# Attention in a hybrid block: ACT's casts and bank copies ahead of the exponentials, other places for a modulation sum, for output products and for weight splits

## The chip, the cores and the metric

The kernel runs on 1 core of one Trainium2 chip. The metric is the time of one execution on the device in microseconds (us), median of 3 runs. The engines are named as the profile names them: PE (TensorE, matmuls; PEld its weight loads), DVE (VectorE), ACT (ScalarE), POOL (GpSimd) and SP (SyncE, which issues the DMAs here). Each engine works its own queue in order, and engines wait for one another by semaphores.

## The reference, cut to what matters

One layer of a flow-matching block on 512 latent tokens with 256 context tokens as a prefix, model width 1024, all in float32. The input projection is split into three groups of heads: grouped-query attention, a long convolution, and differential attention.

```python
sh1, sc1, g1, sh2, sc2, g2 = split(silu(c) @ w_mod + b_mod, 6)     # csh1 ... from c_ctx
h  = modulate(rms_norm(x, norm1_g), sh1, sc1);  hc = modulate(rms_norm(ctx, norm1_g), csh1, csc1)
qa, ka, va, hy, qd, kd, vd = split(h @ w_in)                       # and the same of hc
# attention: 4 query heads on 2 key heads; keys and values = context (256) + latent (512) = 768
ya = softmax(qa ka^T / 8) va
# differential attention: 4 heads, two 64-wide halves j, values 128 wide
yd = softmax(q1 k1^T / 8) vd - lam * softmax(q2 k2^T / 8) vd
yh = hyena(hy)                                                     # long convolutions
y  = concat(rms_norm(ya), rms_norm(yh), rms_norm(yd) per head * 0.2) @ w_out
x  = x + g1 * y
x  = x + g2 * conv_glu(modulate(rms_norm(x, norm2_g), sh2, sc2))
```

## The kernel before, in words

Matmuls that need more than one pass's accuracy split both operands into a rounded high part and a low part and add three products (`mm3`): `hi_of` makes the high part by a cast, mostly on ACT, `lo_of` the low part by a subtraction on DVE or POOL.

*Order.* The layer that the kernel is written in plans each engine's order from program order and a planning model. Where the code enters `tc.manual_schedule(engines=...)`, the named engines run the instructions traced inside in exactly the order of the code; instructions traced outside may be planned between them. `tc.issue_after(ins)` queues what is traced in it behind `ins` on the engine of `ins`. Buffers (`bufs=`) of one tag are reused; which one a new tile gets is fixed by the planner, and its first write waits for the last use of the tile before.

*Modulation sums.* The four vectors g1, sh2, sc2, g2 are sums over 8 row blocks of `w_mod`. A call of `mod2_step` (L746) loads one block (512 KB, two buffers) and adds it, scaled, to a running sum on DVE (`macc`, L761, L763). After the eighth block of a group the next call does nothing (`pause`), and the call after that closes the sum first (`due`: 16 small matmuls on PE into `mc`, L768, one add on DVE into `mcol`, L769) and then loads the next group's first block. Calls stand in the loop over the input projection's eight column chunks: `MOD_AT` calls ahead of each half chunk, 22 in all, in chunks 1 to 6 (`ci`), and in the last chunk (`ci == 7`) at places `e` of its twelve groups of matmuls. In the last chunk PE and DVE are ordered by hand, and six early score tiles of head 0 (`early_step`: scores `se`, maximum `mxe`, exponential `pe`) run between the projection's matmuls.

*Attention.* From L1160 a loop runs over steps n. Steps 3 to 15 here are the differential heads (4 heads x 4 query tiles; 0 to 2 were the early ones), 16 to 31 the grouped-query heads. PE, DVE and ACT are ordered by hand. A step below `LATE` = 16 does, in this order: scores of half 0 on PE into one of two score banks `s`, row maximum on DVE, exponential on ACT; `combine` of step n-1 (DVE and POOL mix the two probabilities); `advance`; three transposes of the first half of step n-3's probabilities on PE into one of three banks (`ps_t`), a copy of that bank on ACT (`at`); scores, maximum, exponential of half 1; the other three transposes and their copy; the products with the values of step n-5 (`yd`); `advance` again. `advance` lets each running side job do its next piece: preparing the next head's q and k (transposes `qT`, `kT` on PE, casts `qhl`, `kh` on ACT, low parts on DVE, DMAs that stack them), finishing a head (`ysb`, `natural` = transposes `ynd`, copy, squares, norm), splitting the grouped-query values (`vas`), and writing an output operand (`y_out`: transposes `yT`, cast `Y` on ACT, low part on DVE). These side jobs use the same three transpose banks. In the trace a name such as `Td21` is head 2, query tile 1.

*End of the attention and output projection.* After the loop, `TAIL` says how many output products (`accumulate`, one product = three matmuls of 512 columns into `o`) go to PE ahead of each further `advance`. The advances finish the grouped-query heads: `natural`, scaling (L1022), squares, reduction (L1028), reciprocal root on POOL, scaling of `yna` (L1037), transposes `yTa`, `Y` cast and low part, twice. The 24 products that need neither `Y[0]` nor `Y[1]` are spread over these places; the rest follow at once. Weight units 0 to 7 of `w_out` (`wo_unit`: load `or`, cast `oh` or `ox`, low part `ol` or `ox`) alternate: units 0 to 2 are split during the loop, 3 to 7 are traced behind the hand-ordered part; the letter of `WO_LO` says whether POOL or DVE makes the low part. Loads of raw units share three buffers, which later hold the gate weights `ur` too. Then come g1 spread over the rows (`mr`), the last products, the residual sum on x, the second norm and the gated MLP.

Of the kernel before, what the change touches and what calls it, by code (L numbers as in the profile page):

```python
# [8 lines left out]
F32 = mybir.dt.float32  # L9
F32R = mybir.dt.float32r  # L10
AF = mybir.ActivationFunctionType
ALU = mybir.AluOpType
AX = mybir.AxisListType
# [3 lines left out]
P = 128  # L17
WO_LO = "ppppvvvv"

# [7 lines left out]
WO_AT = (24, 26, 28)  # L27
TAIL = (2, 0, 0, 0, 0, 0, 7, 0, 0, 2)
UP_AT, UP_AHEAD, UP_NEXT, UP_LAG = 4, 5, 5, 2
# [15 lines left out]
def block_kernel(tc, x, ctxt, small, ffs, wmod1, wmod2, whyd, wqkvd, woutd, wupd, wdownd,  # L45
# [700 lines left out]
    def mod2_step():  # L746

        if m2s.pop("pause", False):
            return
# [14 lines left out]
        if k == NK - 1:  # L764
            def due(a=m2s["a"]):
                t0 = m2s["ps"](f"mc{g}")
                for i in range(NK):
                    T_.matmul(t0[:, 2 * i:2 * i + 2], a[:, i * P:(i + 1) * P], ones[:, 0:2], start=True, stop=True)  # L768
                V.tensor_tensor(mcol[:, g], t0[:, 0:16:2], cols[:, C_BM + 8 * g:C_BM + 8 * g + 8], ALU.add)  # L769
            m2s["due"], m2s["pause"] = due, True  # L770

    def scores(s, qs, ks, kz, j, tt):

        q2 = qs[:, j, tt * P:(tt + 1) * P]
        for c0, c1 in ((0, 512), (512, 768)):
            T_.matmul(s[:, c0:c1], q2, ks[j][:, c0:c1], start=True, stop=False)
            T_.matmul(s[:, c0:c1], q2, kz[j][:, c0:c1], start=False, stop=True)

    def exp_of(p_, mx, s, stat):
        V.tensor_reduce(mx, s[:, :768], AX.X, ALU.max, negate=True)  # L780
        S.activation(p_, s[:, :768], AF.Exp, bias=mx, scale=1.0, accum_out=stat)
# [10 lines left out]
    def early_step(e):  # L792
        n, jj = divmod(e, 2)
        if n >= EARLY:
            return
        qs, (ks, kz) = prepared[0]["q"], prepared[0]["k"]
        s = pp(f"se{n}{jj}")
        scores(s, qs, ks, kz, jj, n)
        if jj:
            p_ = big(f"pe{n}{jj}")[:, :768]  # L800
        else:
            p_ = f(rows_of(y_tile(f"pe{n}{jj}"), 768))
            held[n] = []
        mx = cst.tile([P, 1], F32, tag="mxe", bufs=2, name=f"mxe{n}{jj}")
        exp_of(p_, mx, s, state["st0"][:, n, jj:jj + 1])
        held[n].append(p_)
# [10 lines left out]
    for ci, ch in enumerate(corder):  # L817
# [6 lines left out]
        for u in range(2):  # L824
# [8 lines left out]
            for b, bank in enumerate(banks):  # L833
                th, tl = (hTh, hTl) if b < 2 else (cTh, cTl)
                for j in range(2):
# [6 lines left out]
                    if ci == 7:  # L842
# [3 lines left out]
                        if e in (4, 8):  # L846
                            early_mix(e // 4 - 1)
                        if e % 3 == 0:
                            mod2_step()
# [164 lines left out]
    def finish_a(b, yps):  # L1014
# [15 lines left out]
        if b == 1:  # L1030
# [4 lines left out]
            for b_ in range(2):  # L1035
                yv = yna[b_].rearrange("p a j d -> p a (j d)")
                V.tensor_tensor(yv, yv, sa[:, 2].unsqueeze(2).broadcast_to([P, 4, P]), ALU.mult)  # L1037
                yield
                yield from y_out(b_, f"a{b_}", lambda tt: yv[:, tt])
# [7 lines left out]
    def front(n, jj):  # L1047
# [3 lines left out]
        if kind == "a":  # L1051
            if jj:
                return lambda: []
            stat, j_ = sta[:, tt, 2 * h + j:2 * h + j + 1], j
# [8 lines left out]
        def rest():  # L1063
            mx = att.tile([P, 1], F32, tag="mx", bufs=4, name="mx" + nm)
            p_ = att.tile([P, 768], F32, tag="p", bufs=7, name="p" + nm)
            exp_of(p_, mx, s, stat)
            return [p_]
        return rest
# [61 lines left out]
    def wo_unit(n_):  # L1130
# [9 lines left out]
        hi_of(h, r, "a")  # L1140
        lo_of(l, r, h, WO_LO[n_])
        wo[n_] = h.rearrange("p (k c) -> p k c", k=2), l.rearrange("p (k c) -> p k c", k=2)
# [22 lines left out]
    while n < len(steps) + D_V:  # L1165
# [10 lines left out]
        if late:  # L1176
# [4 lines left out]
            if n - 1 in waiting:  # L1181
                held[n - 1] = waiting.pop(n - 1)()
            if on(D_C):
# [8 lines left out]
        else:  # L1192
            held[n] = front(n, 0)()
            if on(D_C):
                combine(n - D_C, held[n - D_C])
            advance()
            if on(D_T):
                transposes(n - D_T, held[n - D_T][0], 0)
            held[n] += front(n, 1)()
            if on(D_T):  # L1200
                transposes(n - D_T, held.pop(n - D_T)[0], 1)
            if on(D_V):
                values(n - D_V)
# [303 lines left out]
```

## Time and profile before

| | before |
|---|---|
| median of 3 runs | 807.86 us (805.63 to 809.38) |
| the profiled execution: its time | 807.56 us |
| the profiled execution: span, first to last instruction | 805.8 us |
| PE busy | 774.5 us (96%) |
| DVE, ACT, POOL busy | 476.9, 317.8, 194.6 us |

The profile is of one execution. Its span is 1.8 us shorter than that execution's time. A busy PE is not PE at its peak, but where PE is not busy it waits, and the rows of the trace name for whom. Times in the rows are microseconds from the start of the span.

### The profile page before, as it was taken

What the parts mean: (1) busy time and instruction counts of PE and PEld (TensorE: products, weight loads), DVE (VectorE), ACT (ScalarE), POOL (GpSimd) and SP (SyncE); (2) the same over time, 40 slices, a digit from 0 to 9 for tenths busy, and PEclk for the clock granted to TensorE, in tenths of its full rate; (3) what the DMA queues carried; (4) which work ended last, traced back from release to release, by engine and by line L of the source; (5) the groups of instructions that cost most, each with busy time, mean ns of one, the idle gap of its engine ahead of it and who ended that gap; (6) DMA issues with size and microseconds to landing.
All of it is one profiled execution on the core that took longest, in us unless ns stands there. A gap on an engine that the chain in (4) does not pass through costs nothing.

```text
span 805.8 us, 11143 instructions
## 1 busy us (share of the span) xinstructions
PE 774.5 (96%) x4355; PEld 655.1 (81%) x4355; DVE 476.9 (59%) x683; ACT 317.8 (39%) x546; POOL 194.6 (24%) x187
## 2 busy tenths in 40 slices
PE   8899999999989888899899999999999999999997
PEld 2278899999988777789689988888888888888886
DVE  5588659687767777776476785344444433332325
ACT  2576343223213678787243343323333332332220
POOL 0518036849821657421151000000000000000000
PEclk9799999999999999999999999999999999999999
DMA  8913311225675241501551372322232222223202
GB/s 325 393 51 112 105 54 53 79 79 179 214 218 161 66 104 29 144 27 53 171 171 54 113 245 86 105 104 83 101 105 90 93 99 84 100 85 104 79 27 104
DMA packets 30701, 93.68 MB, mean 116 GB/s; under 512 B 5639, under 2 KB 8022, under 8 KB 29625
## 3 DMA queue, kind: packets, MB, share of 16 engines
q1 hardware_dynamic: 30649, 92.98, 35.0%
q8 instruction: 34, 0.56, 0.3%
q14 instruction: 18, 0.15, 0.1%
HBM read 83.79 MB, written 2.10 MB: 107 GB/s over the span
## 4 chain that ended last, share of the span: by engine, by line
PE 81%; DVE 6%; DMA 4%; ACT 4%; POOL 2%; issue 1%; SPq 0%; ACTq 0%; DVEq 0%; POOLq 0%
PE u L84 5%; PE u L83 5%; PE u L85 5%; PE dn L85 5%; PE dn L84 5%; PE dn L83 5%; DMA mraw<-in_dram 4%; PE uv L83 2%; PE ua L85 2%; PE uv L84 2%; PE uv L85 2%; PE ua L83 2%; PE ua L84 2%; PE yd L1103 2%; PE o L85 2%; PE o L84 2%
## 5 line engine op out<-in xcount | busy, mean ns | idle before, releaser
L80 DVE TENSOR_TENSOR ul<-ur,uh 128x1024 fp32r<-128x1024 f32 x62 | 75.9, 1224 | 101.6 <-ACT uh L72 100.9
L72 ACT CAST uh<-ur 128x1024 fp32r<-128x1024 f32 x66 | 69.2, 1051 | 116.8 <-PE u L84 90.6
L83 PE MATMUL u<-h2h,uh 128*128 128x512 f32 (+1 forms) x224 | 81.3, 363 | 0.0
L85 PE MATMUL u<-h2h,ul 128*128 128x512 f32 (+1 forms) x224 | 80.4, 359 | 0.0
L84 PE MATMUL u<-h2l,uh 128*128 128x512 f32 (+1 forms) x224 | 80.4, 359 | 0.0
L84 PE MATMUL dn<-ul,gh 128*128 128x512 f32 x176 | 69.6, 397 | 0.0
L85 PE MATMUL dn<-uh,gl 128*128 128x512 f32 x176 | 69.6, 397 | 0.0
L83 PE MATMUL dn<-uh,gh 128*128 128x512 f32 x176 | 69.3, 397 | 0.0
L80 DVE TENSOR_TENSOR gl<-gT,gh 128x512 fp32r<-128x512 f32 x22 | 15.2, 690 | 60.1 <-ACT gh L72 60.1
L84 PEld LDWEIGHTS u<-h2l,uh 128*128 128x128 f32 x224 | 42.3, 189 | 6.3
L83 PEld LDWEIGHTS u<-h2h,uh 128*128 128x128 f32 x224 | 42.3, 189 | 6.2
L85 PEld LDWEIGHTS u<-h2h,ul 128*128 128x128 f32 x224 | 42.3, 189 | 6.2
L80 DVE TENSOR_TENSOR wl<-wr,wh 128x1024 fp32r<-128x1024 f32 x22 | 31.5, 1433 | 19.4 <-ACT wh L72 19.3
L763 DVE SCALAR_TENSOR_TENSOR macc<-mraw,sv,macc 128x1024 f32<-128x1024 f32 x28 | 37.4, 1335 | 8.1 <-DMA mraw<-in_dram 8.0
L72 ACT CAST gh<-gT 128x512 fp32r<-128x512 f32 x22 | 13.5, 620 | 70.1 <-PE dn L84 70.1
L83 PEld LDWEIGHTS dn<-uh,gh 128*128 128x128 f32 x176 | 33.2, 189 | 8.1
L85 PEld LDWEIGHTS dn<-uh,gl 128*128 128x128 f32 x176 | 33.2, 188 | 8.1
L84 PEld LDWEIGHTS dn<-ul,gh 128*128 128x128 f32 x176 | 33.2, 188 | 8.0
L72 ACT CAST wh<-wr 128x1024 fp32r<-128x1024 f32 x22 | 23.0, 1047 | 41.2 <-PE hy L84 8.2
L83 PE MATMUL uv<-h2h,uh 128*128 128x512 f32 x80 | 31.2, 391 | 0.2 <-ACT uh L72 0.2
L83 PE MATMUL ua<-h2h,uh 128*128 128x512 f32 x80 | 31.4, 392 | 0.0
L84 PE MATMUL uv<-h2l,uh 128*128 128x512 f32 x80 | 31.2, 390 | 0.0
(771 smaller groups left out, 2173.9 us busy)
## 6 DMA issues: line engine op xcount, KB each, us to landing
ur<-in_dram SPq DMA_DIRECT2D x66, 512.0 KB, 3.2
mraw<-in_dram SPq DMA_DIRECT2D x32, 512.0 KB, 4.5
wr<-in_dram SPq DMA_DIRECT2D x22, 512.0 KB, 3.3
mraw<-in_dram SPq DMA_DIRECT2D x8, 1024.0 KB, 11.8
or<-in_dram SPq DMA_DIRECT2D x8, 512.0 KB, 4.6
xo<-in_dram SPq DMA_DIRECT2D x6, 512.0 KB, 9.3
x<-in_dram SPq DMA_DIRECT2D x4, 512.0 KB, 5.8
out_dram<-x SPq DMA_DIRECT2D x8, 256.0 KB, 2.0
```

What stands on the lines that cost most here:

```text
L72: return S.copy(dst, src)
L80: return e.tensor_tensor(dst, src, f(hi), ALU.subtract)
L83: i0 = T_.matmul(o, ah, bh, start=start, stop=False)
L84: T_.matmul(o, ah, bl, start=False, stop=False)
L85: return i0, T_.matmul(o, al, bh, start=False, stop=stop)
L763: V.scalar_tensor_tensor(m2s["a"], r, sv[:, k:k + 1], m2s["a"], ALU.mult, ALU.add)
L1103: T_.matmul(o, Vt[2 + h][:, kt], at[:, kt], start=kt == 0, stop=kt == 5)
```

## The change

Five edits. (1) In steps 3 to 15 the maximum and the exponential are taken apart: the maximum is issued with the scores, the first exponential behind `advance` and the first copy of the transpose bank, the second exponential behind the second copy. Steps from 16 on keep their order. (2) After the second modulation sum two calls do nothing in place of one; in the last chunk the calls stand at e = 2, 4, 6, 8, 9 in place of 0, 3, 6, 9. (3) `TAIL` puts ten products in place of seven ahead of the first `yTa` transposes and four in place of two ahead of the second. (4) The low part of output weight unit 3 is made on DVE in place of POOL. (5) The low parts of units 4 to 7 on DVE are queued behind the last scaling of `yna`.

```diff
-WO_LO = "ppppvvvv"
+WO_LO = "pppvvvvv"
...
-TAIL = (2, 0, 0, 0, 0, 0, 7, 0, 0, 2)
+TAIL = (2, 0, 0, 0, 0, 0, 10, 0, 0, 4)
...
     def mod2_step():
-        if m2s.pop("pause", False):
+        if m2s.get("pause"):
+            m2s["pause"] -= 1
             return
...
-            m2s["due"], m2s["pause"] = due, True
+            m2s["due"], m2s["pause"] = due, 2 if g == 1 else 1
...
+    def max_of(mx, s):
+        V.tensor_reduce(mx, s[:, :768], AX.X, ALU.max, negate=True)
+
     def exp_of(p_, mx, s, stat):
-        V.tensor_reduce(mx, s[:, :768], AX.X, ALU.max, negate=True)
         S.activation(p_, s[:, :768], AF.Exp, bias=mx, scale=1.0, accum_out=stat)
...
-                        if e % 3 == 0:
+                        if e in (2, 4, 6, 8, 9):
                             mod2_step()
...
-                V.tensor_tensor(yv, yv, sa[:, 2].unsqueeze(2).broadcast_to([P, 4, P]), ALU.mult)
+                state["yna"] = V.tensor_tensor(yv, yv, sa[:, 2].unsqueeze(2).broadcast_to([P, 4, P]), ALU.mult)
...
         def rest():
             mx = att.tile([P, 1], F32, tag="mx", bufs=4, name="mx" + nm)
-            p_ = att.tile([P, 768], F32, tag="p", bufs=7, name="p" + nm)
-            exp_of(p_, mx, s, stat)
-            return [p_]
+            max_of(mx, s)
+
+            def exps():
+                p_ = att.tile([P, 768], F32, tag="p", bufs=7, name="p" + nm)
+                exp_of(p_, mx, s, stat)
+                return [p_]
+            return exps
         return rest
...
-        lo_of(l, r, h, WO_LO[n_])
+        if n_ < 4:
+            lo_of(l, r, h, WO_LO[n_])
+        else:
+
+            with tc.issue_after(state["yna"].ins):
+                lo_of(l, r, h, WO_LO[n_])
...
-                held[n - 1] = waiting.pop(n - 1)()
+                held[n - 1] = waiting.pop(n - 1)()()
...
-            held[n] = front(n, 0)()
+
+            exps = front(n, 0)()
             if on(D_C):
                 combine(n - D_C, held[n - D_C])
             advance()
             if on(D_T):
                 transposes(n - D_T, held[n - D_T][0], 0)
-            held[n] += front(n, 1)()
+            held[n] = exps()
+            exps = front(n, 1)()
             if on(D_T):
                 transposes(n - D_T, held.pop(n - D_T)[0], 1)
+            held[n] += exps()
             if on(D_V):
                 values(n - D_V)
```

## Rows read from the trace of the kernel before

**Rows 1.** Busy time by stretch: from:to, length, five engines, PEclk (1.00 full), DMA

```profile
240.00:242.00 2.00, 2.00 (x12) 2.00 (x11) 0.87 (x1) 0.04 (x1) 0.00 (x0) 0.50 0.80 260
268.00:340.00 72.00, 61.51 (x375) 53.50 (x375) 53.35 (x99) 53.27 (x118) 44.44 (x36) 1.00 0.34 85
378.00:392.00 14.00, 11.70 (x67) 9.53 (x66) 6.64 (x9) 3.80 (x5) 3.61 (x3) 1.00 0.22 75
402.00:806.00 404.00, 399.08 (x1858) 330.92 (x1856) 190.07 (x234) 127.35 (x174) 14.15 (x12) 1.00 0.30 102
```

**Rows 2.** Waits of PE, 268 to 340: waiter, releaser: us in total, times, longest

```profile
PE Td03None L1086 <- ACT atd02None L72: 1.8, 1, 1.8
...
PE sd10None L776 <- ACT pd03None L781: 0.8, 1, 0.8
...
PE Td30None L1086 <- DVE kzY L80: 0.2, 1, 0.2
```

**Rows 3.** Timeline of ACT in step 12: start, us, line, operation, out<-in [idle before <-releaser]

```profile
308.70 0.90 ACT L781 ACTIVATE pd30None<-sd30None,mxd30None 128x768 f32<-128x768 f32 x1 [0.61 <-DVE rrd L784]
...
309.59 0.68 ACT L978 ACTIVATE Y<-yTd,cols 128x512 fp32r<-128x512 f32 x1
310.15 0.58 ACT L72 CAST qhla<-qTa 128x512 fp32r<-128x512 f32 x1
310.62 0.50 ACT L72 COPY atd20None<-Td21None 128x384 f32<-128x384 f32 x1
310.99 0.93 ACT L781 ACTIVATE pd30None<-sd30None,mxd30None 128x768 f32<-128x768 f32 x1
```

**Rows 4.** Timeline of PE in step 12: transposes, the last score matmul, transposes

```profile
308.32 0.49 PE L1086 MATMUL Td21None<-ident,pd21None 128*128 128x128 f32 x3
...
309.22 0.28 PE L777 MATMUL sd30None<-X,X 128*128 128x256 f32 x1
311.17 0.55 PE L1086 MATMUL Td21None<-ident,pd21None 128*128 128x128 f32 x3 [1.67 <-ACT atd20None L72]
```

**Rows 5.** Timeline of PE and ACT in step 13 and at step 14's scores

```profile
313.88 0.60 PE L960 MATMUL ynd<-ident,ysbd 128*128 128x128 f32 x4
...
315.69 0.47 ACT L72 CAST kha<-kT0a 128x384 fp32r<-128x384 f32 x1
...
317.94 0.47 ACT L72 COPY atd22None<-Td22None 128x384 f32<-128x384 f32 x1
...
318.20 0.59 PE L776 MATMUL sd32None<-ksX,X 128*128 128x512 f32 x1
```

**Rows 6.** Timeline at the attention's end, POOL, DVE, ACT, PE; one matmul from the chain

```profile
382.08 2.41 POOL L80 TENSOR_TENSOR ol<-or,oh 128x1024 fp32r<-128x1024 f32 x1 [15.92 <-ACT oh L72]
382.98 2.59 DVE L80 TENSOR_TENSOR ol<-or,oh 128x1024 fp32r<-128x1024 f32 x1
383.09 0.63 ACT L1026 ACTIVATE ysqa<-yna 128x512 f32<-128x512 f32 x1
385.50 0.67 DVE L1028 TENSOR_REDUCE sa<-ysqa 128x4 f32<-128x512 f32 x1
388.61 0.63 PE L971 MATMUL yTa<-ident,yna 128*128 128x128 f32 x4 [1.44 <-DVE yna L1037]
391.49 0.63 PE L971 MATMUL yTa<-ident,yna 128*128 128x128 f32 x4 [0.85 <-DVE yna L1037]
392.35 0.24 PE o L84
399.57 1.23 DVE L80 TENSOR_TENSOR ol<-or,oh 128x1024 fp32r<-128x1024 f32 x1 [5.94 <-ACT oh L72]
```

**Rows 7.** Timeline in the last chunks of the input projection, PE and DVE

```profile
236.49 1.92 PE L768 MATMUL mc<-ones,macc 128*128 128x2 f32 x16 [2.11 <-DVE macc L763]
...
249.25 1.28 DVE L763 SCALAR_TENSOR_TENSOR macc<-mraw,sv,macc 128x1024 f32<-128x1024 f32 x1 [1.46 <-DMA mraw<-in_dram]
...
252.54 0.50 PE L776 MATMUL se<-ks0d,qsd 128*128 128x512 f32 x1 [1.05 <-ACT pe L781]
```

More of the change, by code (lines that the diff above doesn't have):

```diff
@@ L1052, in front @@
             if jj:
-                return lambda: []
+                return lambda: lambda: []
             stat, j_ = sta[:, tt, 2 * h + j:2 * h + j + 1], j
@@ L1064, in rest @@
             mx = att.tile([P, 1], F32, tag="mx", bufs=4, name="mx" + nm)
-            p_ = att.tile([P, 768], F32, tag="p", bufs=7, name="p" + nm)
-            exp_of(p_, mx, s, stat)
-            return [p_]
+            max_of(mx, s)
+            def exps():
[3 more added lines that the diff above has]
+            return exps
         return rest
```

## The prediction, made before the changed kernel was run

> **What bounds the kernel now.** I read the busy time of stretches first, then who TensorE (PE) waits for in the stretches where it is not full, then the queues of the engines it waits for, row by row. From 402 us to the end PE is busy for 399.08 of 404.00 us, so the kernel is bound by PE there and whatever is won earlier is kept. In the attention stretch from 268 to 340 us PE is busy for only 61.51 of 72.00 us while ACT and DVE are each near 53, and at the end of the attention, 378 to 392, for 11.70 of 14.00 [rows 1]. So the change has 10.5 us to win in one place and 2.3 us in the other. The waits of PE in 268 to 340 are thirteen rows, from 1.8 to 0.2 us [rows 2]. Eight of them (1.8, 1.7, 1.2, 1.2, 1.1, 0.7, 0.6, 0.4, together 8.7) are transposes that wait for a cast or copy on ACT which frees a bank; three (0.8, 0.3, 0.2) are scores that wait for an exponential.
>
> **Part 1, ACT's order in steps 3 to 15.** Nothing is added or removed; the first exponential of a step goes behind the step's casts and the first bank copy, the second behind the second copy. One step worked out: step 12 (head 3, query tile 0). ACT now does the exponential at 308.70, then the Y cast at 309.59, the q cast at 310.15, the bank copy at 310.62 until 311.12 [rows 3]. PE finished the first transposes of that step at 308.32 + 0.49 = 308.81 and had nothing to do after 309.22 + 0.28 = 309.50; the second transposes start at 311.17, having waited 1.67 for that copy [rows 4]. In the new order the copy stands behind the Y cast (0.56) and the q cast (0.47), and not behind the exponential. If both casts have still to run when its input is there, it runs from 309.84 to 310.34 and the wait shrinks by 0.8; if they are done, it ends at 309.31, before PE needs it, and the whole 1.67 goes. Their inputs come from transposes ahead of these on PE, so I take 80%, nearer the second end. For the eight waits: 8.7 x 0.8 = 7.0 us won, bounds 4.4 (half) and 8.7.
>
> Against it stands that the exponentials come later, and they free the two score banks. In step 13 four casts stand ahead: 315.69 to 317.94, or 2.25 us [rows 5]. They can start about when the head's natural-layout transposes end, 313.88 + 0.60 = 314.48, so the copy comes at some 316.7, the exponential at 317.1 (the copy occupies ACT for 0.37, from 310.62 to 310.99 [rows 3]) and its bank is free at 318.0 with 0.89 for the exponential (308.70 to 309.59). The next scores on PE start at 318.20 now and would want to start at 317.0, since 1.2 of wait goes in this very step: a new wait of about 1.0 [rows 5]. In a step without casts the exponential comes later by the copy at most, 0.37; over 13 steps that is 4.8, if none of it is covered. So the new waits lie between 1.0 and 1.0 + 4.8 = 5.8. I take 2.0: the step with most casts in full and a fifth of the copies, because the exponential waits for its maximum on DVE anyway in most plain steps. Sum of part 1: -7.0 + 2.0 = **-5.0 us**, bounds -7.7 and +1.4 (ends against ends). POOL's mixing of two probabilities follows the second exponential and is used three steps later; that distance covers a shift below 1 us, and a slip beyond it would cost PE as much. The casts' own DMAs on SP, which stack the next head's q and k, start earlier; no row of PE waits for one now, so that is worth 0.
>
> [...]
>
> **Part 2, the end of the attention.** PE waits 1.44 us before the first yTa transposes and 0.85 before the second; both waits are for DVE's scaling of yna [rows 6]. One output product is three matmuls of 0.23 to 0.24, or 0.70 [rows 6]. Three more of them ahead of the first wait are 2.1 us, above 1.44, two more ahead of the second are 1.4, above 0.85. They are moved, not added: the rest that follows is five shorter. So both waits are filled, -2.3, even if the chain on DVE keeps its pace. The chain itself should gain: the reduction at 385.50 had its input at 383.09 + 0.63 = 383.72 and stood behind the subtraction of weight unit 4, 382.98 for 2.59 [rows 6]. That one now goes behind the last yna scaling. Unit 3's subtraction comes from POOL (382.08, 2.41) to DVE, where one alone takes 1.23 [rows 6]. If the planner puts it ahead of the reduction, the reduction starts at 384.2 at the earliest. At worst it adds 1.23 to the chain with no gain: then 1.44 + 1.23 - 2.1 = 0.6 of waiting stays and the part gives -1.7. **-2.3 us**, bounds -2.3 and -1.7.
>
> What is late next: unit 4's low half comes behind the second yna scaling, which ends just ahead of the second yTa at 391.49, so some 8 us later. Its products start only after eight remaining products (5.6 us) and eight more with unit 3; a slip beyond that cover would stall PE by the slip. The load of unit 7 waits for unit 4's raw buffer and may stand ahead of the four x loads on SP's queue. I cost both at nothing: x is used after the eight and the first four of the products with unit 3, 8.4 us, unit 7 later still. POOL loses unit 3's subtraction and then holds only the chain's own two small steps.
>
> **Part 3, the modulation sums.** The second sum is closed at call 20 in place of 19. Both calls stand in one loop with nothing traced between them, so its closing matmuls (236.49, after 2.11 of waiting [rows 7]) keep their place: 0. What moves is the loads and sums after it, one call later, and in the last chunk they are called at 2, 4, 6, 8, 9 in place of 0, 3, 6, 9. There PE waited 1.05 for the second early exponential; its maximum stood behind a sum at 249.25 that waited 1.46 for its load [rows 7]. With calls at 2 and 4 no hand-placed sum lies between the first two maxima: up to -1.05. But five sums now share that region in place of four, two of them in successive calls near its end, ahead of the last maximum; one late load there costs up to the same 1.46. I take **-0.3**, bounds -1.05 and +1.5; a loss at the end of the region meets the start of step 3, which waits for DVE.
>
> Sum: -5.0 - 2.3 - 0.3 = -7.6. The profiled execution took 807.56 (span 805.8 and 1.8 around it), 0.3 below the median of the runs, 807.86. **Forecast 800.0.**
>
> **Rivals.** *The closing wait goes as well.* [...] 800.0 - 3.1 = 796.9. Against: the order of the code, above. Chance 0.08.
> *Late exponentials eat the gain.* With new waits at their upper bound, 5.8, part 1 gives -7.0 + 5.8 = -1.2: 807.56 - 1.2 - 2.3 - 0.3 = 803.8. For it: two score banks only, three waits on exponentials already today. Against: plain steps have no such wait now. Chance 0.17.
> *Slower: ACT's queue stalls in every cast step.* Six of the thirteen steps carry two casts or more by the code. If each delays its first exponential as step 13 does, 2.25 us, with nothing covering it, and the other seven by 0.37, that is 13.5 + 2.6 = 16.1 against 7.0 won: 807.56 + 9.1 - 2.3 - 0.3 = 814.1. [...] Chance 0.05.
> *The change doesn't do what it says.* Which of the three transpose banks a transpose gets is fixed by the planner. If the second transposes get a bank that DVE's low half frees and not ACT's copy, the waits stay: 807.56 - 2.3 - 0.3 = 805.0. Against: rows 2 name ACT as the releaser. Chance 0.08.
>
> **How the numbers follow.** Forecast 0.62, rivals 0.08, 0.17, 0.05, 0.08. A measurement tells about 0.5% from no change, 4.0 us: under 803.8 is faster, over 811.9 slower. Faster: 0.62 + 0.08 + half of 0.17 = 0.78; slower 0.05; the rest, 0.17, within. The forecast's own range has part 1 between -7.0 + 1.0 = -6.0 and, with half of the copies uncovered, -7.0 + 1.0 + 2.4 = -3.6; with parts 2 and 3 at their bounds that is 807.56 - 9.35 = 798.2 to 807.56 - 3.8 = 803.8. The range reaches on to the first rival and past the second, 796.9 to 804.2, and leaves out the last two rivals and the far ends of part 1's bounds, some 0.17.
>
> **What would show it.** Right: PE busy in the attention stretch above 0.92 of it; no wait of a second transpose above 0.6; new waits of scores for exponentials, the largest in step 14; no wait before yTa, and one DVE subtraction of 1.2 there; the closing matmuls still waiting near 2. Wrong: transposes that wait for DVE, exponentials whose wait is named after casts, or PE waiting for a weight unit or an x add after 400.

## The result: 797.49 us, 10.4 us faster

| | before | after |
|---|---|---|
| median | 807.86 us | 797.49 us (796.62 to 799.10) |
| ratio, with its 95% interval | | 0.9880 (0.9865 to 0.9895) |
| the profiled execution: time, span | 807.56, 805.8 us | 796.76, 795.0 us |
| PE busy | 774.5 us (96%) | 771.1 us (97%) |
| DVE, ACT, POOL busy | 476.9, 317.8, 194.6 us | 475.6, 318.2, 193.8 us |

The forecast was 800.0, in a range of 796.9 to 804.2. The direction and the order of the parts were right; the gain was 2.5 us larger than forecast. In a second comparison the changed kernel's ratio was 0.9878 (0.9855 to 0.9901).

Busy time of the changed kernel by stretch (from:to, length, five engines, PEclk, DMA). The lines answer to [rows 1]; the stretches lie 2 to 11 us earlier than there.

```profile
237.00:240.00 3.00, 3.00 (x16) 3.00 (x16) 2.07 (x3) 0.00 (x0) 0.00 (x0) 0.51 0.56 195
266.00:332.00 66.00, 61.33 (x372) 52.77 (x371) 52.69 (x100) 54.29 (x120) 44.48 (x36) 1.00 0.37 93
370.00:384.00 14.00, 14.00 (x76) 11.78 (x75) 5.48 (x10) 3.81 (x5) 1.20 (x2) 1.00 0.11 37
392.00:795.00 403.00, 398.27 (x1854) 330.19 (x1852) 188.77 (x234) 126.88 (x174) 14.14 (x12) 1.00 0.31 104
```

The work of the attention stretch is the same (61.33 and 61.51 us of PE), done in 66 us in place of 72: a busy share of 0.93 in place of 0.85. The attention's end is full. Behind it nothing changed. What PE still waits for from 262 to 340 (waiter, releaser: us in total, times, longest) answers to the thirteen rows of [rows 2]:

```profile
PE yTd L975 <- ACT atd30None L72: 1.6, 1, 1.6
PE sd10None L777 <- ACT pd03None L784: 0.9, 1, 0.9
PE sd32None L777 <- ACT pd31None L784: 0.7, 1, 0.7
PE sd11None L777 <- ACT pd10None L784: 0.6, 1, 0.6
PE Td03None L1094 <- ACT atd02None L72: 0.3, 1, 0.3
PE Td02None L1094 <- ACT atd02None L72: 0.3, 1, 0.3
PE Td21None L1094 <- ACT atd20None L72: 0.2, 1, 0.2
```

**Where the time went, stage by stage.** The span was cut at matmuls that both kernels have: A from the start to the first `hy`, B to the first matmul of chunk 6 (`q6L`), C to the first of chunk 7 (`q7L`), D to the first scores of step 3 (`sd03`), E to the first of step 16 (`sa`), F to the last `yna` transposes, G to the first `dn`, and the rest, to the last row of PE (4.5 us ahead of the end of the span in both). Each number is the difference of two start times in the timeline of PE, in us:

| | A | B | C | D | E | F | G | rest |
|---|---|---|---|---|---|---|---|---|
| before | 57.08 | 162.09 | 22.56 | 26.63 | 62.37 | 50.94 | 295.77 | 123.86 |
| after | 56.13 | 162.10 | 22.28 | 25.19 | 56.89 | 50.91 | 293.13 | 123.86 |
| difference | -0.95 | 0.01 | -0.28 | -1.44 | -5.48 | -0.03 | -2.64 | 0 |

Part 1 of the prediction lies in E, part 2 in G, part 3 in C, D and the start of E. Stage A is not touched by the change. This cut is more exact than the medians: over the kernels below, stages that an edit does not touch repeat within 0.2 us, except A (56.0 to 57.2, once 61.6) and C (20.1 to 24.2), which hang on loads (in the changed kernel PE waited 8.3 us for loads in A, and the last addition ahead of the closing matmuls in C 0.86 for its load), and E where the clock fell in it (e5 and the repeat, below).

### The profile page after: what moved, and what is told of

Its sections match the earlier page's. It is cut to its first block, busy times and chain, and to the rows that moved or that the text cites. A ratio compares the mean times of both kernels' runs of the same rounds, so it can differ in the third digit from the quotient of the medians.

```text
span 795.0 us, 11146 instructions
## 1 busy us (share of the span) xinstructions
PE 771.1 (97%) x4355; PEld 654.2 (82%) x4355; DVE 475.6 (60%) x684; ACT 318.2 (40%) x546; POOL 193.8 (24%) x186
## 4 chain that ended last, share of the span: by engine, by line
PE 84%; DVE 5%; DMA 4%; ACT 3%; POOL 2%; issue 1%; SPq 0%; DVEq 0%; ACTq 0%; POOLq 0%
PE u L84 5%; PE u L85 5%; PE u L83 5%; PE dn L85 5%; PE dn L84 5%; PE dn L83 5%; DMA mraw<-in_dram 4%; PE uv L83 2%; PE ua L85 2%; PE uv L84 2%; PE uv L85 2%; PE ua L83 2%; PE ua L84 2%; PE yd L1111 2%; PE o L85 2%; PE o L84 2%
## 5 line engine op out<-in xcount | busy, mean ns | idle before, releaser
L80 DVE TENSOR_TENSOR wl<-wr,wh 128x1024 fp32r<-128x1024 f32 x22 | 31.6, 1434 | 19.3 <-ACT wh L72 19.2
```

The lines of the kernel that those rows point to most:

```text
L80: return e.tensor_tensor(dst, src, f(hi), ALU.subtract)
```

## Experiments

### Each edit alone

The first four kernels are the kernel before with one edit each (e4 with two); e1 is the order of ACT (edit 1).

```diff
-            held[n] = front(n, 0)()
+            exps = front(n, 0)()
...
+            held[n] = exps()
...
-            held[n] += front(n, 1)()
+            exps = front(n, 1)()
...
+            held[n] += exps()
```

> The kernel before with the order of ACT in steps 3 to 15 alone changed (edit 1). Theory, from matching the PE instructions of the two traces: the lead of the changed kernel grows by 5.8 us between step 3 and the last grouped-query products, and all of it is this edit, so this kernel is 5.8 us faster than before (ratio 0.9928), its waits on bank copies in that stretch fall from about 8.7 to under 3 us, and the two yTa waits stay at 1.4 and 0.9. Rival: a part of the 5.8 comes from the earlier start of the stage after the modulation edit; then this kernel gains 4 us or less.

Measured: 801.65 us, ratio 0.9921 (0.9902 to 0.9941); stage E 56.08 in place of 62.37, so 6.3 us, and all of it in this stage. Three of its waits of PE from 262 on:

```profile
PE yTa L974 <- DVE yna L1040: 2.3, 2, 1.5
PE yTd L974 <- ACT atd30None L72: 1.7, 1, 1.7
PE sd32None L776 <- ACT pd31None L783: 0.7, 1, 0.7
```

The theory holds, with 6.3 in place of 5.8: the yTa waits stay, and the waits on copies are those of the changed kernel, 2.5 in sum (1.7, 0.3, 0.3, 0.2).

e2 is edit 2 alone.

```diff
-            m2s["due"], m2s["pause"] = due, True
+            m2s["due"], m2s["pause"] = due, 2 if g == 1 else 1
...
-                        if e % 3 == 0:
+                        if e in (2, 4, 6, 8, 9):
```

> The kernel before with the modulation edit alone (edit 2). Theory: the lead that the changed kernel has at the last scores ahead of step 3 beyond the 0.9 us that it already had at 60 us, 1.5 us, comes from this edit: 0.5 at the closing matmuls mc and 1.0 at the second early exponential; ratio 0.9981. Rival 1: the 0.5 at mc is a load that landed early by chance; then mc waits near 2.1 again and the gain is 1.0. Rival 2: my forecast, 0.3, is right and the rest was chance as well; ratio 0.9996.

Measured: 806.41 us, ratio 0.9989 (0.9971 to 1.0007): not told from no change. The stages tell more: D is 25.22 in place of 26.63, and E is 63.27 in place of 62.37. So the last chunk wins 1.4 and the first attention steps give 0.9 back, a net gain of 0.5. The closing matmuls waited 1.74; in e1, e3, e4 and e5, which have the old places, they waited 2.63, 1.85, 1.20 and 1.82, so the 0.5 that the changed kernel seemed to win there was a load's chance: rival 1 is right on that. Neither the theory nor the rivals had the loss in E.

e3 is edit 3 alone, `TAIL` with 10 and 4; e4 is edits 4 and 5 alone, the other places of the weight splits.

```diff
-TAIL = (2, 0, 0, 0, 0, 0, 7, 0, 0, 2)
+TAIL = (2, 0, 0, 0, 0, 0, 10, 0, 0, 4)
```

> The kernel before with ten and four output products in place of seven and two (edit 3 alone). Theory: both yTa waits (1.44 and 0.85) go, and with each the 0.17 us by which a matmul of 0.40 overlaps the next at a spacing of 0.23, so 2.6 us faster, ratio 0.9968. Rival: the waits go only together with the other place of the weight splits, because DVE's chain is what is long; then the wait before the first yTa stays at 0.6 or more and the gain is below 1.7.

```diff
-WO_LO = "ppppvvvv"
+WO_LO = "pppvvvvv"
...
-        lo_of(l, r, h, WO_LO[n_])
+        if n_ < 4:
+            lo_of(l, r, h, WO_LO[n_])
+        else:
+            with tc.issue_after(state["yna"].ins):
+                lo_of(l, r, h, WO_LO[n_])
```

> The kernel before with the low part of weight unit 3 on DVE and those of units 4 to 7 behind the last scaling of yna (edits 4 and 5 alone). Theory: DVE's chain to the first yTa gets 0.6 us shorter (the reduction no longer stands behind a subtraction, 1.8 less, but a subtraction of 1.2 comes ahead of the first scaling), so the first yTa wait falls from 1.4 to 0.8 and the time by 0.6 us, ratio 0.9993. Rival: the first scaling is ahead of the subtraction here, and the chain gains 1.8; then the wait goes and the gain is 1.4 to 1.6.

Measured for e3: 804.38 us, ratio 0.9951 (0.9932 to 0.9970); stage G 293.16, 2.6 less, and no wait of PE at the end of the attention. For e4: 806.20 us, ratio 0.9982 (0.9966 to 0.9999); stage G 294.91, 0.9 less. Its yTa waits, 1.44 and 0.85 before [rows 6]:

```profile
385.23 0.63 PE L971 MATMUL yTa<-ident,yna 128*128 128x128 f32 x4 [0.58 <-DVE yna L1037]
388.11 0.63 PE L971 MATMUL yTa<-ident,yna 128*128 128x128 f32 x4 [0.86 <-DVE yna L1037]
```

So e3's theory holds, and e4's 0.9 lies between its theory (0.6) and its rival (1.4 to 1.6), nearer the theory. Together the two give no more than e3 alone (2.64 in the changed kernel, 2.61 in e3): ten and four products cover the waits of DVE's longer chain already, and the other places of the splits are worth nothing beside them. Added up, the edits' effects in the stages are 6.3 + 1.4 - 0.9 + 2.6 = 9.4 us, inside the interval of the result (8.5 to 10.9). The profiled pair differs by 10.8 because of stages A and C, which move from run to run whatever the edit.

### Which of the two exponentials

e5 moves the first exponential of a step and leaves the second ahead of the second copy.

```diff
-            held[n] = front(n, 0)()
+            exps = front(n, 0)()
...
-            held[n] += front(n, 1)()
+            held[n] = exps()
+            held[n] += front(n, 1)()()
             if on(D_T):
                 transposes(n - D_T, held.pop(n - D_T)[0], 1)
```

> The kernel before with only the first exponential of each step 3 to 15 moved (behind the casts and the first bank copy); the second stays ahead of the second copy. Theory: the long waits were of second transposes for the first copy, so the first exponential carries most of it: the stage from the first scores of step 3 to the first scores of step 16, 62.4 us before and 56.1 with both moved, takes 57.5 or less, and the waits that stay longest are those of transposes that open a step. Rival: the second exponential carries as much, since its copy frees the bank for the next step's side transposes; then the stage takes 59 or more.

Measured: 803.21 us in its one run; stage E 58.98, 3.4 less than before and 2.9 more than with both moved. By the number that lies between the theory's 57.5 and the rival's 59, and nearer the rival. But nearly all of the 2.9 is one place, ACT in step 15 and PE in step 16 (the last two lines: the stretch behind it, and the same six products in e1):

```profile
320.85 0.90 ACT L783 ACTIVATE pd33None<-sd33None,mxd33None 128x768 f32<-128x768 f32 x1 [2.95 <-DVE rrd L786]
...
321.99 0.90 ACT L783 ACTIVATE pd33None<-sd33None,mxd33None 128x768 f32<-128x768 f32 x1
...
322.88 0.47 ACT L72 COPY atd30None<-Td30None 128x384 f32<-128x384 f32 x1
...
323.40 1.11 PE L974 MATMUL yTd<-ident,ynd 128*128 128x128 f32 x4 [3.03 <-ACT atd30None L72]
324.31 2.39 PE L1110 MATMUL yd<-atd22None,vd 128*128 128x256 f32 x6
...
322.78:326.19 3.41, 2.79 (x9) 2.41 (x10) 1.77 (x3) 2.01 (x6) 3.14 (x3) 0.50 0.20 82
...
323.08 1.46 PE L1110 MATMUL yd<-atd22None,vd 128*128 128x256 f32 x6
```

The second copy stands behind two exponentials, of which the first waits 2.95 us for DVE; ACT does nothing in that time and lets no later instruction through: the transposes that it copies, the second of Td30, had ended at 318.42 (317.93 + 0.49), and the copy ran at 322.88. With both exponentials moved the wait of yTd is 1.65, with the first alone 3.03, in the kernel before 0.71.

At the end of the wait of 3.03 and behind it the granted clock was 0.50 for 3.41 us (322.78 to 326.19), and six products that take 1.46 in e1 took 2.39. Set beside e1 matmul by matmul from the first scores of step 3 on, e5 is 0.2 later just ahead of this wait, 1.55 at yTd and 2.9 at the first scores of step 16: 1.4 is the longer wait, 1.35 the lower clock behind it. So outside this one place the second exponential carries 0.2, and without the fall of the clock E would have been about 57.6 (an estimate, 58.98 - 1.35), close to the theory's 57.5. The number alone pointed to the rival.

### The three places where PE still waits

v1 puts both exponentials of step 15 behind both copies, in the changed kernel.

```diff
-            held[n] = exps()
-            exps = front(n, 1)()
+            both = n == LATE - 1
+            if not both:
+                held[n] = exps()
+            exps1 = front(n, 1)()
             if on(D_T):
                 transposes(n - D_T, held.pop(n - D_T)[0], 1)
-            held[n] += exps()
+            if both:
+                held[n] = exps()
+            held[n] += exps1()
```

> The changed kernel with one more move: in step 15 alone both exponentials stand behind both bank copies. In the changed kernel the second copy of that step stands behind the first exponential, which waits 2.94 us for its maximum, and the transposes yTd of step 16 wait 1.65 for that copy. Theory: that order is the cause, so the wait goes and the stage from step 3 to step 16's first scores, 56.9, takes 55.2 (1.65 of wait less, or 1.8 with the overlap of two matmuls). Rival: DVE is what is late there, and the wait moves to the next maximum or exponential; then under 0.5 is won by the 20 us behind it.

Measured: 800.22 us in its one run, which says little here, since its stage A took 61.61. E is 55.03, 1.9 less, and F is 52.68, 1.8 more. The wait moved, as the rival said, and came back as one for POOL:

```profile
326.44 0.87 PE L1094 MATMUL Td32None<-ident,pd32None 128*128 128x128 f32 x6 [1.12 <-POOL pd32None L790]
...
323.57 0.91 POOL L789 TENSOR_SCALAR pd32None<-pd32None,mld 128x768 f32<-128x768 f32 x1 [3.12 <-DVE mld L788]
```

POOL's mixing and the exponential hang on the same late maximum on DVE. So the order of ACT was only where that lateness showed. In the changed kernel that maximum comes at 318.53, behind three operations on DVE of which one, a scaling of 128x4, took 1.12 us from 315.79 (last section).

v2 starts the split of the grouped-query values a step later; v4 takes the longer pause back and keeps the new places.

```diff
-VA_AT = 13
+VA_AT = 14
```

> The changed kernel with the split of the grouped-query values one step later, so that step 13 has three casts ahead of its first copy in place of four (one of 0.81 us less) and step 15 gets one. Theory: the new wait of step 14's scores, 0.73 us, is the price of casts ahead of an exponential, so it shrinks by the cast to nothing, and the changed kernel's 56.9 us stage becomes 56.2. Rival: the exponential itself is late by its maximum; then the wait stays above 0.5. A loss is possible in step 15, where the cast of 0.8 comes ahead of the copies whose bank already is waited for 1.65.

Measured: 798.39 us in its one run; PE no longer waits at step 14's scores, and E is 56.09, 0.8 less. The theory holds to 0.1: the price of a cast ahead of this exponential was the cast, where the scores want the bank.

```diff
-            m2s["due"], m2s["pause"] = due, 2 if g == 1 else 1
+            m2s["due"], m2s["pause"] = due, 1
```

> The changed kernel without the longer pause: the second sum is closed one call earlier, as before, and the new places in the last chunk stay. Theory: the new places bring the 1.4 us that the last chunk got shorter by (26.6 to 25.2 from its first matmul to step 3), and the pause, which puts a fifth sum at the end of the chunk, two in a row ahead of the last maximum, costs what step 3 and 4 gave back, 0.9 (56.1 to 56.9). So the last chunk takes 25.2 again and the stage after it 56.1: 0.8 us better than the changed kernel. Rival: without the pause the sums ahead of the second early maximum are two again and it waits for a load: then the last chunk takes 26 or more.

Measured: 796.78 us in its one run; D 25.33, E 56.41. Of the 0.8 by which the changed kernel's E is above e1's, 0.5 is the pause's, for 0.1 in D: the sign of the theory, half of its size. The other 0.3 comes in at one place, the first scores of step 11, where v4 too falls 0.3 behind e1: an exponential of step 10 ahead of them starts 0.3 later there, and why it does was not tried.

v6 joins the two and scales each finished head on DVE one turn later.

```diff
         rstd_of(s4[:, 2], s4[:, 0], P, 4)
         yield
         yield
+        yield
         V.scalar_tensor_tensor(s4[:, 2], s4[:, 2], 1.0 - LAM_INIT, ...)
         V.tensor_tensor(v4(yn), v4(yn), ...)
         yield
         yield
-        yield
         yield from y_out(4 + h, ...)
```

> The changed kernel with three moves: the split of the grouped-query values a step later, the pause of the second sum back to one call, and the scaling of each finished head on DVE half a step later (one more turn ahead of it, one less behind it). In the changed kernel the maximum of step 15 starts at 318.53 though its scores end at 315.67, because DVE is held by the two operations of that scaling; both the exponential ahead of the copy that yTd waits for, and POOL's mixing for Td32, hang on that maximum. Theory: with the scaling behind the maximum both are 1.6 us earlier, the yTd wait of 1.6 goes and no wait of Td32 comes in its place, so the two stages from the last chunk to the end of step 16's region take 25.3 + 56.9 - 0.7 (no wait in step 14) - 0.3 (pause) - 1.6 = 79.6 in place of 82.1, and the time is 2.5 below the changed kernel's. Rival: the scaling is then late for yTd itself, or its place in the other heads costs as much; then the sum stays above 81.

The changed kernel, run beside it:

> The changed kernel once more, beside the next two on the same chip. By the stages of the traces the change is worth 6.3 (the order of ACT) less 0.5 to 0.9 that the modulation edit gives back behind it, 1.4 in the last chunk, and 2.6 at the end: 9.4 to 9.8 in all, ratio 0.988. Its stages should repeat within 0.3 us: last chunk to step 3 25.2, step 3 to step 16 56.9, and only the start and the wait for the last load of the second sum should differ.

Measured: v6 795.49 us, ratio 0.9867 (0.9845 to 0.9889); the changed kernel 796.74 us, 0.9878 (0.9855 to 0.9901). By the stages v6 is 1.7 us shorter than the changed kernel in D to F (25.27 + 54.73 + 51.29 against 25.19 + 56.89 + 50.91), D and E together 80.0 where the theory said 79.6. The medians, 1.25 us apart, do not tell the two kernels apart. Its largest waits from 262 to 340, and DVE in steps 14 and 15:

```profile
PE yTd L975 <- ACT atd30None L72: 0.7, 1, 0.7
...
PE Td32None L1094 <- POOL pd32None L790: 0.5, 1, 0.5
```

```profile
314.77 1.92 DVE L80 TENSOR_TENSOR vas<-va,vas 128x768 fp32r<-128x768 f32 x1
316.72 0.96 DVE L781 TENSOR_REDUCE mxd33None<-sd33None 128x1 f32<-128x768 f32 x1
```

The maximum comes at 316.72 in place of 318.53. The wait of yTd is 0.7 in place of 1.65, and Td32, which waited 1.12 for POOL in v1, waits 0.5. The maximum would be earlier still, had the low part ahead of it not taken 1.92 (below).

The repeat of the changed kernel kept D (25.19) but E was 57.60, 0.7 more than in the first profile and more than the 0.3 expected. The clock is the reason: it was 0.61 of full in 266 to 270, and the second matmuls of the scores there took 0.63 in place of 0.39. That cost 1.2, of which 0.6 fell into the wait of step 4's scores (0.2 in place of 0.9).

### The closing matmuls of the second sum

The prediction's first rival was that their wait goes. It did not in the changed kernel, so v7 makes it go: v6 with five calls of pause and the next sum's calls at the places 1 to 8 of the last chunk.

```diff
-            m2s["due"], m2s["pause"] = due, 1
+            m2s["due"], m2s["pause"] = due, 5 if g == 1 else 1
...
-                        if e in (2, 4, 6, 8, 9):
+                        if 1 <= e <= 8:
```

> The kernel of the run before with the second sum closed in the last chunk (five calls of pause, the eight calls of the next sum at the places 1 to 8). This is the first rival of the prediction, made to happen: the closing matmuls stand a few us later, where the sum has long been ready. Theory: their wait (1.6 in the changed kernel, 1.1 to 2.7 in the runs) goes, and the 3.3 us at the granted clock of 0.50 behind it, which cost 1.6 of work, too; 3.2 us less from the second half of chunk 6 to the end of the last chunk. Rival: eight loads in 25 us, two buffers, take DVE's queue at its maxima, and the early exponentials come late; each load that is late by 1 us costs as much, and nothing is left of the gain.

Measured: 799.29 us, ratio 0.9905 (0.9881 to 0.9928): 3.8 above v6's median of the same runs, the two intervals just meeting, and from B to the last row of PE 739.0 us in the profiles against v6's 732.8 (v7's profile is of the slowest of its six runs, 802.41, so it shows the loss larger than the medians do). Both sides are right. C took 17.18 in place of v6's 22.36: 5.2 less, of which 1.8 are the closing matmuls that moved on to D, so 3.3 won, as expected. D took 35.50 in place of 25.27, and E 55.81 in place of 54.73. Two sums on DVE and two early scores on PE from its timeline, then one stretch with the clock (columns as above):

```profile
251.46 1.69 DVE L764 SCALAR_TENSOR_TENSOR macc<-mraw,sv,macc 128x1024 f32<-128x1024 f32 x1 [2.44 <-DMA mraw<-in_dram]
...
260.27 1.28 DVE L764 SCALAR_TENSOR_TENSOR macc<-mraw,sv,macc 128x1024 f32<-128x1024 f32 x1 [2.23 <-DMA mraw<-in_dram]
...
257.28 0.50 PE L777 MATMUL se<-ks0d,qsd 128*128 128x512 f32 x1 [2.50 <-ACT pe L784]
264.71 0.80 PE L777 MATMUL se<-ks1d,qsd 128*128 128x512 f32 x1 [3.30 <-ACT pe L784]
```

```profile
263.43:277.08 13.65, 12.37 (x50) 11.61 (x50) 8.14 (x15) 4.50 (x10) 7.83 (x6) 0.50 0.04 11
```

Late loads hold DVE's queue, the maxima come late, PE waits 2.5 and 3.3 us for exponentials, and from 263.4 to 277.1, into step 4, its granted clock was 0.50. Set beside v6 matmul by matmul, v7 falls back by 3.4 more in D behind the second of these waits and by 1.1 in E: 4.5 of the 11.3 us that D and E lose came with the lower clock.

v8 goes the other way: v6 with all modulation calls half a chunk earlier.

```diff
-MOD_AT = (0, 0, 0, 2, 2, 2, 2, 2, 2, 2, 2, 2, 2, 2, 0, 0)
+MOD_AT = (0, 0, 2, 2, 2, 2, 2, 2, 2, 2, 2, 2, 2, 0, 0, 0)
```

> The kernel with the later scaling (the run of that name), and in it the calls that load and add the modulation blocks begin and end half a chunk of the input projection earlier; nothing is added. In all runs so far the closing matmuls of the second sum waited 0.8 to 2.7 us for its last addition, which waited for its load; where they waited 1.2 or more, a stretch of about 3 us at the granted clock of 0.50 followed, where 0.8 or 1.1 the clock stayed at 1.00. Theory: the loads are what is late there, so half a chunk earlier (some 10 us) they are in time, the wait and the slow stretch go, and the stage from the first matmul of chunk 6 to the first of chunk 7 takes 19.2 in place of 20.0 to 24.2, without the late loads that the close in the last chunk brought: 2 to 3 us below the kernel it is made from. Rival: the loads then take the DMA engines from the weight loads of the chunk before, and PE waits for a weight cast instead; then the stage ahead of it, 162.1 in every run, grows by as much.

Measured: 799.17 us, ratio 0.9898 (0.9877 to 0.9919); from B to the last row of PE 735.8, 3.0 above v6. The closing matmuls wait for nothing, and C took 20.21 (with 1.0 of head 0's transposes, which the planner moved into it from B: 19.2 without). The rival's wait did not come; another did, and D took 31.42 in place of 25.27:

```profile
244.68 0.76 PE L777 MATMUL se<-ks0d,qsd 128*128 128x512 f32 x1 [5.14 <-DMA ks0d<-khd]
```

The planner now puts head 0's transposes at 232.90 in place of 217.43. Its low parts on DVE start at 237.05, behind a sum that waits 1.55 for its load. The DMAs that stack its keys are issued from 238.91 on, the first lands 4.8 us later, and the first scores of the last chunk start 5.1 us late. From 241.9, within that wait, to 248.7 the granted clock was 0.50. Neither of the two places tried for the close beats that of the change: in both the wait of the closing matmuls went, and a DMA that came late behind the move, with the lower clock behind that, cost more.

## Why the prediction was right, point by point

**Part 1: mechanism right, both terms forecast too large, so that their errors nearly cancel.** Forecast -7.0 + 2.0 = -5.0; measured -6.3. Step 12, which the prediction worked out, in the changed kernel (ACT, PE):

```profile
303.25 0.58 ACT L72 CAST qhla<-qTa 128x512 fp32r<-128x512 f32 x1
303.72 0.49 ACT L72 COPY atd20None<-Td21None 128x384 f32<-128x384 f32 x1
304.09 0.93 ACT L784 ACTIVATE pd30None<-sd30None,mxd30None 128x768 f32<-128x768 f32 x1
...
304.26 0.55 PE L1094 MATMUL Td21None<-ident,pd21None 128*128 128x128 f32 x3 [0.17 <-ACT atd20None L72]
```

The wait of 1.67 [rows 4] is 0.17: nearer the end at which all of it goes. Over the eight waits 8.7 became 2.4, so 6.3 and not 7.0 were won, and one row makes the difference: seven fell from 8.0 to 0.7, and the eighth, yTd in step 16, rose from 0.7 to 1.65. (One of the seven, ynd with 0.6, waits for its own input, a copy on ACT, and not for a bank; it went with the others.) The prediction took one share for all waits; in step 15 the exponential that now stands ahead of the second copy is itself held up by DVE:

```profile
319.58 0.90 ACT L784 ACTIVATE pd33None<-sd33None,mxd33None 128x768 f32<-128x768 f32 x1 [2.94 <-DVE rrd L787]
...
320.99 0.66 PE L975 MATMUL yTd<-ident,ynd 128*128 128x128 f32 x4 [1.65 <-ACT atd30None L72]
```

By its words, "no wait of a second transpose above 0.6", the prediction's sign is met; this wait of a side transpose is the one above it.

The second term was forecast as 1.0 in step 14 and 1.0 in the plain steps. Step 13 in the changed kernel:

```profile
308.82 0.81 ACT L72 CAST vas<-va 128x768 fp32r<-128x768 f32 x1
309.54 0.47 ACT L72 COPY atd22None<-Td22None 128x384 f32<-128x384 f32 x1
309.91 0.90 ACT L784 ACTIVATE pd31None<-sd31None,mxd31None 128x768 f32<-128x768 f32 x1
...
310.95 0.51 PE L777 MATMUL sd32None<-ksX,X 128*128 128x512 f32 x1 [0.73 <-ACT pd31None L784]
```

The new wait is in the place forecast, step 14, and 0.73. In the plain steps only sd11 grew, from 0.3 to 0.6. So 1.0 in place of 2.0; a fifth of the copies uncovered was still too much. And three small waits of [rows 2] that the prediction left alone (0.4 for POOL, 0.2 and 0.2) went too. That is -6.3 + 1.0 - 0.8 = -6.1 of the 6.3 measured in e1; the last 0.2 is not traced to rows. So the gain was forecast 0.7 too large and the loss 1.0 too large, which nearly cancels by luck, and the 1.3 missed is mostly in waits to which the prediction gave no term.

**Part 2: right.** Forecast -2.3, measured -2.6. Both waits are gone, and DVE's one subtraction of 1.23 stands ahead of the first scaling:

```profile
373.87 1.23 DVE L80 TENSOR_TENSOR ol<-or,oh 128x1024 fp32r<-128x1024 f32 x1 [3.46 <-ACT oh L72]
376.45 0.69 DVE L1032 TENSOR_REDUCE sa<-ysqa 128x4 f32<-128x512 f32 x1 [0.76 <-ACT ysqa L1030]
378.74 0.69 DVE L1041 TENSOR_TENSOR yna<-yna,sa 128x512 f32<-128x512 f32 x1 [1.41 <-POOL sa L196]
...
380.93 0.60 PE L975 MATMUL yTa<-ident,yna 128*128 128x128 f32 x4
384.87 0.60 PE L975 MATMUL yTa<-ident,yna 128*128 128x128 f32 x4
```

The scaling ends at 379.43, 1.5 ahead of the transposes. The 0.3 beyond the two waits is the overlap: a matmul of 0.39 was followed by the next after 0.23 (377.67, 377.90), and this 0.16 is lost once for each wait (2.29 + 2 x 0.16 = 2.61). e4 shows that the other places of the splits shorten the chain by the 0.9 that the prediction's 'the chain itself should gain' meant, and e3 that nothing of it is needed. No wait for a weight unit or an x add came: stage G is 2.64 shorter, all of it at its start.

**Part 3: right in sum, of two terms that work against each other.** Forecast -0.3, measured -0.5. The closing matmuls kept their place, as the order of the code said, and their wait changes with the loads: 0.85 to 2.68 in twelve profiles, the kernel before, the changed one and its repeat among them, without a difference that their spread would let one see (mean 1.9 of five with the old places, 1.6 of seven with the new). In the last chunk the 1.05 went, as the prediction's bound had it, and with the overlap lost beside it that one place gave 1.3 of the 1.4. What was left over is the prediction's 'a loss at the end of the region meets the start of step 3':

```profile
260.15 1.28 DVE L764 SCALAR_TENSOR_TENSOR macc<-mraw,sv,macc 128x1024 f32<-128x1024 f32 x1
261.68 1.61 DVE L764 SCALAR_TENSOR_TENSOR macc<-mraw,sv,macc 128x1024 f32<-128x1024 f32 x1
264.35 0.96 DVE L781 TENSOR_REDUCE mxe<-se 128x1 f32<-128x768 f32 x1
...
269.27 0.50 PE L777 MATMUL sd10None<-ksX,X 128*128 128x512 f32 x1 [0.92 <-ACT pd03None L784]
```

Two sums stand ahead of the last early maximum, and PE comes to step 3 1.4 us earlier than it did, DVE does not. Of the 0.9 given back, 0.5 is lost by step 4: 0.3 ahead of the second half of step 3's scores (1.35 us behind the first half, 1.05 before) and 0.2 at step 4, whose wait of 0.92 was 0.76 before. This part is gone in v4, so it is the pause's. The other 0.3 is in step 11 (v4, above), which no term of the prediction covers.

**The sum.** Of the 2.5 us between forecast and result, the stages hold 1.8: 9.4 in place of 7.6, of which 1.3 in part 1, 0.3 in part 2 and 0.2 in part 3. The remaining 0.7 is less than stages A and C move by themselves.

**The rivals.** *The closing wait goes as well*, 796.9, is nearest to the measured time, and it is not what happened: the wait is there in both profiles of the changed kernel (1.56 and 0.85). A time alone would have pointed to the wrong case. The 3.1 that it takes off is an estimate, the wait of 2.11 [rows 7] and half of the 2.0 us at a granted clock of 0.50 in 240 to 242 [rows 1]. No run shows this term; the trace of the kernel before has 3.4 us at 0.50 (238.9 to 242.3), and in v7, where the wait went, 3.3 was won in its place, against v6, whose wait was 1.64. That is close to 3.1, partly by luck. *Late exponentials eat the gain* is wrong: new waits of 1.0, not 5.8. *ACT's queue stalls in every cast step* is wrong for most steps, and right for step 13 (0.73, where the prediction estimated 1.0) and, with an exponential ahead of a copy, for step 15. *The change doesn't do what it says* is wrong: the copies still release the second transposes.

## What to carry to other kernels

A queue that runs in order, as ACT's did in e5, is best sorted by who needs the result first, not by when it was traced: a copy that frees a bank for PE in this step belongs ahead of an exponential that POOL needs in the next one (6.3 us in e1). Before giving all waits of a kind the same share, look in each step whether the instruction that now goes first is itself late; in the step where it is, the wait grows, and the lower clock at a longer wait (0.50 for 3.41 us at the wait of 3.03 in e5) may be read as part of the edit's effect. And where one edit moves several stages, cut the traces at matmuls that both kernels have: most stages repeated within 0.2 us where whole runs of one kernel lay 2.5 to 7.4 us apart, so the 1.4 won and the 0.9 given back by the modulation edit could be seen, though its time could not be told from no change.

## What the runs showed of the hardware

**The clock behind a wait.** Behind the closing matmuls of the second sum the granted clock fell in some runs and not in others. Waits of 0.85 (the repeat of the changed kernel) and 1.11 (v1) left it at 1.00 throughout 232 to 262; after 1.20 (e4) it was 0.50 from 237.6 to 241.0, and after 1.56 it was 0.51 in 237 to 240 (first fence). Stage C was 22.28 with the wait of 1.56 and 20.05 with that of 0.85: with 0.7 more of wait it took 2.2 us more, two thirds of it through the clock (an estimate, 2.2 - 0.7). The wait is not the whole of it: waits of 1.8 and 1.7 in the attention of the kernel before left the clock at 1.00 [rows 1], [rows 2], and in the repeat the clock fell in step 3, behind the closing matmuls of the third sum, though PE's longest wait in the 10 us ahead was under 0.3. What else it hangs on is left open. The repeat, behind its closing matmuls of the second sum and in step 3:

```profile
236.00:237.00 1.00, 1.00 (x10) 1.00 (x10) 0.23 (x2) 0.00 (x0) 0.00 (x0) 1.00 0.88 332
266.00:270.00 4.00, 3.82 (x18) 3.13 (x18) 2.20 (x3) 2.57 (x6) 3.59 (x4) 0.61 0.00 0
```

**DVE beside POOL.** The same operation on DVE took up to twice as long, and a small one seven times as long, where POOL was mixing two probabilities: the low part of `vas` 1.92 in v6 (314.77) and 0.95 in the changed kernel, the 128x4 scaling ahead of step 15's maximum 1.12 in the changed kernel (315.79, POOL mixing from 315.05 to 316.89) and 0.15 at 329.54, the last sum 1.61 in place of 1.28, and POOL's mixing beside that sum 2.67 in place of 1.82. POOL in the changed kernel:

```profile
262.30 2.67 POOL L790 TENSOR_TENSOR pe<-pe,pe 128x768 f32<-128x768 f32 x1
```

And POOL in v6, beside that low part:

```profile
314.03 1.85 POOL L790 TENSOR_TENSOR pd31None<-pd31None,pd31None 128x768 f32<-128x768 f32 x1
```

In v6 DVE's low part ends at 316.69, 0.8 after POOL's mixing at 315.88: 0.8 is about what is left of 0.95, so it looks as if DVE had mostly stood still beside POOL and run after it. That is an estimate from these four times; no run shows what held DVE up. The pair at 262 is less clear: there the sum started first, and both took longer, the sum by 0.33 and the mixing by 0.85. A run that takes POOL's mixing away from there was not made. The maxima, which read the score banks, took 0.94 to 0.96 wherever one alone was read, also where POOL was mixing (0.96 from 286.62, POOL from 285.28 to 287.12, in the changed kernel).
